# Attention with unscaled P and 1/sum broadcast through DRAM, in a one-core block of attention, RWKV-7 and a conv-FFN

## The chip, the cores and the metric

One core of a Trainium2 chip runs the whole kernel. The metric is the device time of one execution in microseconds; less is better. The engines are TensorE (PE, matmuls; PEld is its weight load), VectorE (DVE), ScalarE (ACT), GpSimd (POOL) and SyncE (SP, which here only issues DMAs). Each runs its own list of instructions in order, and waits at an instruction until what it needs is there.

## The reference

A block of a language model with 1024 tokens, width 1024, batch 1. What matters here is the mixer:

```
u = modulate(rms_norm(x), shift1, scale1)
proj = u @ w_in                                # fox: q, k, v, f | rwkv | 2 x 1024 gate columns
# 8 heads of 64
logits = q k^T * 64**-0.5 + cum[q] - cum[k]    # causal; cum = cumsum(log_sigmoid(f + b))
probs  = softmax(logits)
o_fox  = probs @ v
o_rwkv = rwkv7_time_mix(...)
merged = sigmoid(gate_fox) * (o_fox @ fox_w_out) + sigmoid(gate_rwkv) * (o_rwkv @ rwkv_w_out)
h = x + gate1 * (merged @ w_o)
u2 = modulate(rms_norm(h), shift2, scale2)
out = rms_norm(h + gate2 * conv_ffn(u2))
```

All in fp32.

## The kernel before

Products of fp32 matrices are made from a high and a low part of each operand (tiles `..hi`, `..lo`, type fp32r), in three matmuls: hi x hi, lo x hi, hi x lo. A weight comes by `load_w`: a DMA of 128x1024 into `raw`, a cast to `hi`, and a subtraction for `lo`. A gate (`w_in` 26 to 41, 16 of them) is computed in two halves of 512 tokens, 24 matmuls of 128x512 each, and its sigmoid is stored in DRAM (`d_gate`) until the branch products `br` want it.

The order on TensorE is written by a planner, `Weave`. Chains of work (Python generators) yield the time at which they wish to go on; a model of each engine's load (`weave.now`, `weave.use`) says when that is. Whenever no chain is due, the planner puts in a step of `weave.queue`: one matmul of a gate product. So the gates are the filler: 18 of their 32 halves stand ahead of the attention, 14 within it. `weave.late` is 0 before the attention, 1 within it, and 2 after. Inside the attention the order on DVE and ACT is that of the code as the planner walks it; SP and POOL are ordered by the scheduler.

In the attention, per head `h`, the queries are eight blocks `i` of 128 and are taken in pairs `I`:

- `load_head` brings three tiles by POOL's DMA queue: `stA` (parts of q and of k, 128 rows), `stB` (the other parts, 68 rows) and `vh` (v, high and low). There are two buffers of each; head 0 is loaded as the section begins, and each next one while its predecessor runs.
- `s_chain` makes the logits `lg` and spawns `softmax`: the negative maximum of a row on DVE (`nm`), Exp on ACT with the row's sum, then on DVE the reciprocal (128x1) and the scaling of P by it.
- `t_chain` transposes P on TensorE (`tp`), `halve` makes `th` (cast, ACT) and `tl` (subtraction, DVE), and `a_chain` multiplies with `vh` into one PSUM tile `ov`.
- `collect` adds the two halves of `ov` into `o` (a COPY on ACT, an addition on DVE). `o` holds two heads in its 128 rows, and 512 queries. When all is there, `fx` (its high and low parts, wanted by `br`) is written, by POOL for the heads 0 to 6, and by ACT and DVE for the last.
- `late_gate` and `gate_out` take one half of a gate at a time in the one PSUM tile `rk_ps`, and end in `gs` (two buffers, tag `sp0`, which the gates ahead of the section use too) and the store to `d_gate`. `weave.hold` keeps the filler away until `rk_ps` is read. The sigmoid is made of Abs, Relu, Exp, Ln, an addition on DVE and Exp, since Exp and Ln are in the table that ACT has loaded.

Later in the program `norm2` (lines L1358 and L1361, with Ln and Exp at L287 and L288) prepares the second norm in two halves; TensorE multiplies with its result `dg` at once (`tr`).

Of the kernel before, what the change touches and what calls it, by code (L numbers as in the profile page):

```python
# [16 lines left out]
S = 1024  # L17
# [114 lines left out]
def hybrid_block(ctx: ExitStack, tc: tile.TileContext, a, out):  # L132
# [41 lines left out]
    ident, ones = f32(eye_r), f32(C("ones"))  # L174
    epsr = cp.tile([128, 3], F32, name="epsr")
    nc.vector.memset(epsr[:, 2:3], 1e-37)
# [26 lines left out]
    d_st = dr.tile([8, 4, 128, S], F32R, name="d_st")  # L203
    d_v = dr.tile([8, 128, 8, 128], F32R, name="d_v")
    d_orw = dr.tile([4, 128, S], F32, name="d_orw")

# [38 lines left out]
    def load_w(src, name, pool=None, n=1024, scale=None, tags=("whi", "wlo"), bufs=2):  # L245

        pool = pool or wp
        raw = rp.tile([128, n], F32, tag="raw", name=f"raw_{name}")
        nc.sync.dma_start(raw, src)
        if scale is not None:  # L250
            nc.gpsimd.tensor_tensor(raw, raw, scale, op=ALU.mult)
        hi = pool.tile([128, n], F32R, tag=tags[0], name=f"hi_{name}", bufs=bufs)
        lo = pool.tile([128, n], F32R, tag=tags[1], name=f"lo_{name}", bufs=bufs)
        if weave.late == 1:
            i = nc.gpsimd.tensor_copy(hi, raw)
            if "head" in marks:
                tc.add_manual_dep(i.ins, marks["head"].ins.name, NOSYNC)
            for c in range(0, n, 256):
                nc.gpsimd.tensor_tensor(lo[:, c : c + 256], raw[:, c : c + 256], f32(hi[:, c : c + 256]), op=ALU.subtract)
        else:  # L260
            nc.scalar.copy(hi, raw)  # L261
            for c in range(0, n, NH):
                nc.vector.tensor_tensor(lo[:, c : c + NH], raw[:, c : c + NH], f32(hi[:, c : c + NH]), op=ALU.subtract)  # L263
        return hi, lo
# [752 lines left out]
    heads = {}  # L1017

    def load_head(h):
        A = at.tile([128, 2, S], F32R, tag="stA", name=f"stA{h}")  # L1020
        nc.gpsimd.dma_start(A, d_st[h, 0:2, :, :].rearrange("k r s -> r k s"))
        B = at.tile([128, 2, S], F32R, tag="stB", name=f"stB{h}")
        nc.gpsimd.dma_start(B[0:68, :, :], d_st[h, 2:4, 0:68, :].rearrange("k r s -> r k s"))
        vh = at.tile([128, 8, 128], F32R, tag="vh", name=f"vh{h}")
        i = nc.gpsimd.dma_start(vh, d_v[h])
        marks.setdefault("head", i)
        heads[h] = A, B, vh

    load_head(0)
    while len(weave.queue) > 12:  # L1030
# [5 lines left out]
    with tc.manual_schedule(engines={mybir.EngineType.DVE, mybir.EngineType.Activation}):  # L1036
        seq = [(h, I) for h in range(8) for I in ((0, 1, 3, 2) if h == 7 else (3, 0, 2, 1))]
        lg_free, tp_free, pl_free, ps_free, th_free, ov_free = (deque([0.0] * n) for n in (2, 2, 4, 2, 3, 1))
        probs, av_queue, halves = {}, deque(), {}
        ov_ps = pb.tile([128, NH], F32, tag="big", name="ov")[:, 0:256]  # L1040
# [7 lines left out]
        def s_chain():  # L1048

            yield 10500  # L1050
            for k, (h, I) in enumerate(seq):
                if k % 4 == 1 and h < 7:
                    load_head(h + 1)
                A, B, _ = heads[h]
                for i in (2 * I, 2 * I + 1):
# [8 lines left out]
                    for c0 in range(0, n, NH):  # L1064
                        c1 = min(n, c0 + NH)
                        mm(lg[:, c0:c1], A[:, 0, qs], A[:, 1, c0:c1], start=True, stop=False)
                        if c1 == n:
                            mm(lg[:, n - 128 : n], eye_r, tri_r, start=False, stop=False)
                        mm(lg[:, c0:c1], B[0:68, 0, qs], B[0:68, 1, c0:c1], start=False, stop=True)
                    weave.spawn(softmax(h, i, n, lg), 351)  # L1070
                    yield 0

        def softmax(h, i, n, lg):
            nm = at.tile([128, 3], F32, tag="nm", name=f"nm{h}_{i}", bufs=4)
            nc.vector.tensor_reduce(nm[:, 0:1], lg[:, 0:n], axis=AX.X, op=ALU.max, negate=True)  # L1075
# [3 lines left out]
            nc.scalar.activation(e[:, 0:n], lg[:, 0:n], AF.Exp, bias=nm[:, 0:1], accum_out=nm[:, 1:2])  # L1079
# [3 lines left out]
            yield t + 140 - weave.now  # L1083
            nc.vector.reciprocal(nm[:, 2:3], nm[:, 1:2])
            ts(e[:, 0:n], e[:, 0:n], nm[:, 2:3], None, op0=ALU.mult)
            t = weave.use("DVE", weave.now, 230 + 0.53 * n)
            probs[h, i] = t + 210, e

        def t_chain():
# [30 lines left out]
        def a_chain():  # L1120

            for _ in range(8 * 10):
# [4 lines left out]
                if jj == 0:  # L1127
                    yield from slot(ov_free)
                vh = heads[h][2]
                order = [(0, th), (1, th), (1, tl), (0, tl)] if jj == I else [(0, th), (0, tl), (1, th), (1, tl)]  # L1130
# [9 lines left out]
        def collect(h, I):  # L1140
# [11 lines left out]
            if len(got) == 4:  # L1152
                cs = slice(hf * NH, hf * NH + NH)
                if h < 7:
                    nc.gpsimd.tensor_copy(fx[0][p][:, cs], o)
                    nc.gpsimd.tensor_tensor(fx[1][p][:, cs], o, f32(fx[0][p][:, cs]), op=ALU.subtract)
                    return
# [8 lines left out]
        def late_gate(w, i):  # L1166
            for hf in range(2):
                cs = slice(hf * NH, hf * NH + NH)
                yield from gemm_steps(rk_ps, w, u, cs)
                weave.hold = weave.now + 1000  # L1170
                pending.append((i, hf))
# [3 lines left out]
        def gate_out(i, hf, cs):  # L1175

            g = gsp.tile([128, NH], F32, tag="sp0", name=f"gs{i}_{hf}")
            m = at.tile([128, NH], F32, tag="gm", name=f"gm{i}_{hf}", bufs=1)
            nc.scalar.activation(g, rk_ps, AF.Abs)
            nc.scalar.activation(m, rk_ps, AF.Relu, scale=-1.0)  # L1180
            weave.hold = weave.use("ACT", weave.now, 960) + 210
            nc.scalar.activation(g, g, AF.Exp, scale=-1.0)
            nc.scalar.activation(g, g, AF.Ln, bias=1.0)
            yield weave.use("ACT", weave.now, 960) + 140 - weave.now
            tt(g, g, m, op=ALU.add)
            yield weave.use("DVE", weave.now, 600) + 140 - weave.now
# [3 lines left out]
            pending.remove((i, hf))  # L1190

        def drain():
# [802 lines left out]
```

## Time and profile before

| what | us |
|---|---|
| median of three runs | 1701.07 (1699.76 to 1704.37) |
| the profiled execution | 1704.73 |
| its span, first to last instruction | 1703.0 |
| its mean granted TensorE clock | 0.983 |
| attention: first matmul into `rk_ps` to first `br` | 656.95 to 868.92 |

The profile is of one execution. Its page gives busy times by engine, the chain of work that ended last, groups of instructions (line, engine, operation, output<-input, shapes, count, then busy time, mean of one in ns, idle time ahead and what ended it) and DMA issues (count, size of one, median time from issue to landing). Other views: waits (engine, its work, what it waited for: total, times, longest), the instructions in order of time (start, length, engine, line, count; in brackets the idle time before it and what ended it) and stretches (for each engine busy time and, in brackets, instructions; then the granted clock of TensorE, the share of the DMA engines and GB/s). Neighbouring matmuls overlap in the listed lengths; their pitch is read from their starts.

### The profile page before, as it was taken

What the parts mean: (1) busy time and instruction counts of PE and PEld (TensorE: products, weight loads), DVE (VectorE), ACT (ScalarE), POOL (GpSimd) and SP (SyncE); (2) the same over time, 40 slices, a digit from 0 to 9 for tenths busy, and PEclk for the clock granted to TensorE, in tenths of its full rate; (3) what the DMA queues carried; (4) which work ended last, traced back from release to release, by engine and by line L of the source; (5) the groups of instructions that cost most, each with busy time, mean ns of one, the idle gap of its engine ahead of it and who ended that gap; (6) DMA issues with size and microseconds to landing.
All of it is one profiled execution on the core that took longest, in us unless ns stands there. A gap on an engine that the chain in (4) does not pass through costs nothing.

```text
span 1703.0 us, 26042 instructions
## 1 busy us (share of the span) xinstructions
PE 1638.0 (96%) x9772; PEld 1342.0 (79%) x9772; DVE 1220.8 (72%) x2390; ACT 808.6 (47%) x1482; POOL 143.4 (8%) x175
## 2 busy tenths in 40 slices
PE   5899999998999998999999999999999999999998
PEld 4767777786877776988878888888888888888886
DVE  5776787778676633888877634897777777787677
ACT  5453334333444554766642323654444444454455
POOL 0010101110111003123112000000000000000000
PEclk8899999999999999999999999999999999999999
DMA  8487743533342326433277611132333233484463
GB/s 328 139 314 205 192 125 97 136 106 106 91 115 75 91 81 151 141 110 107 76 265 268 246 62 63 50 105 94 123 107 103 93 117 101 163 284 153 125 215 112
DMA packets 120974, 239.85 MB, mean 141 GB/s; under 512 B 39888, under 2 KB 48336, under 8 KB 120848
## 3 DMA queue, kind: packets, MB, share of 16 engines
q1 hardware_dynamic: 112896, 220.94, 40.0%
q0 software_dynamic: 7952, 17.25, 3.8%
q8 instruction: 77, 1.26, 0.3%
q14 instruction: 49, 0.40, 0.1%
HBM read 172.59 MB, written 65.54 MB: 140 GB/s over the span
## 4 chain that ended last, share of the span: by engine, by line
PE 79%; DVE 9%; DMA 6%; ACT 2%; issue 2%; SPq 1%; DVEq 0%; ACTq 0%
PE X L140 13%; PE D L140 12%; PE Y L140 6%; PE wo L140 5%; PE br L140 5%; PE gt L140 5%; PE rk_ps L140 4%; PE qk L140 4%; PE ps_rkv L140 4%; PE W L140 3%; PE lg L140 2%; PE v L140 2%; PE ov L140 2%; PE sp L140 2%; PE tp L144 2%
## 5 line engine op out<-in xcount | busy, mean ns | idle before, releaser
L140 PE MATMUL D<-op,op 128*128 128x512 f32 x924 | 209.8, 390 | 0.0
L140 PEld LDWEIGHTS D<-op,op 128*128 128x128 f32 x924 | 173.5, 188 | 36.2 <-DVE op L1258 0.3
L140 PE MATMUL X<-T_m,S 128*128 128x512 f32 x440 | 107.3, 390 | 0.2
L140 PEld LDWEIGHTS X<-T_m,S 128*128 128x128 f32 x440 | 82.5, 188 | 18.2 <-ACT x L1534 0.6
L1257 ACT CAST op<-g 128x512 fp32r<-128x512 f32 x77 | 47.8, 621 | 74.1 <-PE D L140 48.0
L1258 DVE TENSOR_TENSOR op<-g,op 128x512 fp32r<-128x512 f32 x77 | 53.0, 689 | 41.7 <-ACT op L1257 41.7
L1494 DVE SCALAR_TENSOR_TENSOR c<-ab,vec,c 128x512 f32<-128x512 f32 x88 | 65.9, 750 | 19.5 <-ACT c L1497 17.9
L809 DVE TENSOR_TENSOR t<-E,M 128x60 f32<-128x60 f32 (+24 forms) x248 | 57.9, 233 | 30.2 <-DMA M<-sm 24.9
L1458 DVE TENSOR_TENSOR S<-ur,S 128x512 fp32r<-128x512 f32 x66 | 45.5, 691 | 35.6 <-ACT S L1454 35.5
L263 DVE TENSOR_TENSOR lo_in<-raw_in,hi_in 128x512 fp32r<-128x512 f32 x84 | 56.5, 707 | 16.1 <-PE gt L140 13.9
L1454 ACT CAST S<-ur 128x512 fp32r<-128x512 f32 x66 | 41.0, 622 | 55.6 <-DVE ur L1447 30.6
L1458 DVE TENSOR_TENSOR A<-ur,A 128x512 fp32r<-128x512 f32 x64 | 44.1, 688 | 30.9 <-ACT A L1454 30.7
L261 ACT CAST hi_in<-raw_in 128x1024 fp32r<-128x1024 f32 x42 | 44.0, 1049 | 44.3 <-PE ps_rkv L140 16.0
L140 PE MATMUL Y<-T_h,A 128*128 128x512 f32 x264 | 63.5, 390 | 0.0
L140 PE MATMUL Y<-T_h,S 128*128 128x512 f32 x264 | 63.3, 390 | 0.0
L140 PE MATMUL X<-B_b,A 128*128 128x512 f32 x252 | 60.8, 391 | 0.0
L140 PE MATMUL W<-B_f,A 128*128 128x512 f32 x252 | 60.6, 390 | 0.0
L1079 ACT ACTIVATE P<-lg,nm 128x896 f32<-128x896 f32 (+3 forms) x64 | 47.4, 743 | 22.8 <-DVE nm L1075 22.6
L811 DVE TENSOR_TENSOR E<-E,t 128x60 f32<-128x60 f32 (+24 forms) x248 | 53.8, 217 | 5.8
L140 PEld LDWEIGHTS Y<-T_h,A 128*128 128x128 f32 x264 | 49.6, 188 | 10.3
L140 PEld LDWEIGHTS Y<-T_h,S 128*128 128x128 f32 x264 | 49.6, 188 | 10.3
L1454 ACT CAST A<-ur 128x512 fp32r<-128x512 f32 x64 | 39.9, 623 | 34.2 <-PE X L140 31.5
(473 smaller groups left out, 4169.0 us busy)
## 6 DMA issues: line engine op xcount, KB each, us to landing
raw_in<-in_w_in SPq DMA_DIRECT2D x50, 512.0 KB, 3.7
wm<-in_w_mod SPq DMA_DIRECT2D x48, 512.0 KB, 7.0
ur<-in_w_up SPq DMA_DIRECT2D x44, 512.0 KB, 4.2
g<-d_g SPq DMA_DIRECT2D x35, 512.0 KB, 4.0
d_g<-gs SPq DMA_DIRECT2D x44, 256.0 KB, 2.0
d_g<-c SPq DMA_DIRECT2D x33, 256.0 KB, 4.4
d_st<-qh SPq DMA_DIRECT2D x64, 128.0 KB, 2.5
d_gate<-gs SPq DMA_DIRECT2D x32, 256.0 KB, 2.9
```

What stands on the lines that cost most here:

```text
L140: nc.tensor.matmul(o, lhsT, rhs, start=start, stop=stop, skip_group_check=more)
L144: nc.tensor.transpose(o, i, eye)
L261: nc.scalar.copy(hi, raw)
L263: nc.vector.tensor_tensor(lo[:, c : c + NH], raw[:, c : c + NH], f32(hi[:, c : c + NH]), op=ALU.subtract)
L809: tt(tv, E32[:, 0:J, s : s + 1].to_broadcast([128, J, W]), M32[:, s : s + 1, s + 1 : 32].to_broadcast([128, J, W]), op=ALU.mult)
L811: tt(E32[:, 0:J, s + 1 : 32], E32[:, 0:J, s + 1 : 32], tv, op=ALU.add)
L1079: nc.scalar.activation(e[:, 0:n], lg[:, 0:n], AF.Exp, bias=nm[:, 0:1], accum_out=nm[:, 1:2])
L1257: nc.scalar.copy(hi, src)
L1258: tt(lo, src, f32(hi), op=ALU.subtract)
L1454: nc.scalar.copy(hi, src)
L1458: tt(lo, src, f32(hi), op=ALU.subtract)
L1494: stt(c, ab[:, x + hf * NH : x + hf * NH + NH], V("conv_w", 22 * x + i), c, op0=ALU.mult, op1=ALU.add)
```

## The change

Seven edits:

1. `epsr` gets a fourth column that holds 0.5.
2. P stays unscaled. The four sums of a head's half (four blocks) go into one tile `sums`, with one reciprocal of 128x4; SP stores it in DRAM (`d_rs`) with the queries in a row, and loads it back as `R`, 512 queries broadcast to 64 rows. `collect` multiplies `o` by `R` on DVE, once for two heads and 512 queries.
3. A late gate is Tanh(x/2) and Identity(0.5 t + 0.5), both on ACT, and `hold` is 700 in place of 1000.
4. Weights loaded within the attention are split on ACT (cast) and DVE (two subtractions), not on POOL.
5. Head 0 is loaded by five DMAs into tiles of the pool `fxp`, and the two buffers of `stA`, `stB` and `vh` first hold heads 1 and 2; the first logits are due after 3500 ns by the planner's clock, not 10500.
6. POOL writes the low part of `fx` in two pieces of 256 columns.
7. The table of ACT is named ahead of the attention (`exp_and_others`) and after it (`use_ln_exp`).

```diff
@@ load_w
+        nc.scalar.copy(hi, raw)
         if weave.late == 1:
-            i = nc.gpsimd.tensor_copy(hi, raw)
...
-            for c in range(0, n, 256):
-                nc.gpsimd.tensor_tensor(lo[:, c : c + 256], ...)
-        else: ...
+            weave.use("ACT", weave.now, 900)
+            weave.use("DVE", weave.now, 1200)
+        for c in range(0, n, NH):
+            nc.vector.tensor_tensor(lo[:, c : c + NH], raw[:, c : c + NH], f32(hi[:, c : c + NH]), op=ALU.subtract)
@@ load of head 0
+    def load_first():
+        parts = [d_st[0, 0], d_st[0, 1], d_st[0, 2, 0:68, :], d_st[0, 3, 0:68, :], d_v[0].rearrange("p a x -> p (a x)")]
+        tiles = [fxp.tile([128, S], F32R, tag=f"h{t}", name=f"first{t}") for t in (3, 7, 2, 6, 5)]
+        for t, x in zip(tiles, parts):
+            marks["head"] = nc.gpsimd.dma_start(t[0 : x.shape[0], :], x)
+        heads[0] = *tiles[0:4], tiles[4].rearrange("p (a x) -> p a x", x=128)
...
-    load_head(0)
+    load_first()
@@ s_chain
-            yield 10500
+            yield 3500
@@ softmax
+            sm, done = sums[h, hf]
+            nc.scalar.activation(e[:, 0:n], lg[:, 0:n], AF.Exp, bias=nm, accum_out=sm[:, i % 4 : i % 4 + 1])
...
-            nc.vector.reciprocal(nm[:, 2:3], nm[:, 1:2])
-            ts(e[:, 0:n], e[:, 0:n], nm[:, 2:3], None, op0=ALU.mult)
+            if len(done) == 4:
+                nc.vector.reciprocal(sm[:, 4:8], sm[:, 0:4])
+                nc.sync.dma_start(d_rs[h, hf * NH : hf * NH + NH].rearrange("(i k) -> k i", k=128), sm[:, 4:8])
+                if h % 2 == 0:
+                    norms[p, hf] = at.tile([128, NH], F32, tag="R", name=f"R{p}{hf}", bufs=2)
+                nc.sync.dma_start(norms[p, hf][h % 2 * 64 : h % 2 * 64 + 64, :],
+                                  d_rs[h : h + 1, hf * NH : hf * NH + NH].to_broadcast([64, NH]))
@@ collect
             if len(got) == 4:
+                yield t - weave.now
+                tt(o, o, norms[p, hf], op=ALU.mult)
+                t = weave.use("DVE", weave.now, 600) + 140
@@ gate_out
-            nc.scalar.activation(g, rk_ps, AF.Abs)
-            nc.scalar.activation(m, rk_ps, AF.Relu, scale=-1.0)
-            nc.scalar.activation(g, g, AF.Exp, scale=-1.0)
-            nc.scalar.activation(g, g, AF.Ln, bias=1.0)
-            tt(g, g, m, op=ALU.add)
-            nc.scalar.activation(g, g, AF.Exp, scale=-1.0)
+            nc.scalar.activation(g, rk_ps, AF.Tanh, scale=0.5)
+            nc.scalar.activation(g, g, AF.Identity, scale=0.5, bias=epsr[:, 3:4])
@@ around the attention's run
+        nc.scalar.preload_act_table_set("exp_and_others")
         weave.run([a_chain(), t_chain(), s_chain()])
...
+    use_ln_exp()
```

Where the planner and the scheduler put it. First the start of the section on TensorE. A name's number tells buffers apart. Before, gate matmuls lead up to the first logits:

```order
L140 MATMUL rk_ps<-u_hi,hi_in_6764 128x512 x8
L140 MATMUL rk_ps<-u_lo,hi_in_6764 128x512 x8
L140 MATMUL rk_ps<-u_hi,lo_in_6765 128x512 x8
L140 MATMUL rk_ps<-u_hi,hi_in_6764 128x512 x8
L140 MATMUL rk_ps<-u_lo,hi_in_6764 128x512 x8
L140 MATMUL rk_ps<-u_hi,lo_in_6765 128x512 x3
L140 MATMUL lg_6_6952<-stA_6855 128x512
L140 MATMUL lg_6_6952<-stB_6857 128x512
```

Now, at the same place:

```order
L140 MATMUL rk_ps<-u_hi,hi_in_6766 128x512 x8
L140 MATMUL rk_ps<-u_lo,hi_in_6766 128x512 x8
L140 MATMUL rk_ps<-u_hi,lo_in_6767 128x512
L140 MATMUL lg_6_6922<-first_6858,first_6857 128x512
L140 MATMUL lg_6_6922<-first_6860,first_6859 128x512
L140 MATMUL lg_6_6922<-first_6858,first_6857 128x384
```

The logits of head 0 moved ahead by 26 gate matmuls. On ACT the place now reads (L328 is the last function of the last gate ahead of the section):

```order
L328 ACTIVATE gs_1_6886<-gs_1_6886 128x512
L1088 ACTIVATE P_6_6950,sums_1_6951<-lg_6_6922,nm_6_6934 128x896
L1198 ACT_TABLE_LOAD
L1198 ACTIVATE gs_0_6954<-rk_ps 128x512
L1200 ACTIVATE gs_0_6954<-gs_0_6954,epsr 128x512
L1088 ACTIVATE P_7_6958,sums_1_6951<-lg_7_6928,nm_7_6944 128x1024
```

The table comes in with the first Tanh, behind the first Exp of P; the two loads that the new calls name stand at the start of the whole program.

On DVE, the product with R for heads 0 and 1, second half of the queries, and what stands between it and the reciprocal of head 1 (rows left out in the middle are maxima, `tl` and `o` as these):

```order
L1163 TENSOR_TENSOR o_7119<-o_7119,ov 64x256
L1096 RECIPROCAL sums_1_7152<-sums_1_7152 128x4
L1130 TENSOR_TENSOR tl_30_7290<-tp_30_7261,th_30_7274 128x512
L1130 TENSOR_TENSOR tl_31_7294<-tp_31_7267,th_31_7279 128x512
L1130 TENSOR_TENSOR tl_32_7321<-tp_32_7302,th_32_7311 128x512
```

```order
L1130 TENSOR_TENSOR tl_10_7465<-tp_10_7437,th_10_7446 128x512
L1163 TENSOR_TENSOR o_7082<-o_7082,ov 64x256
L1080 TENSOR_REDUCE nm_0_7477<-lg_0_7461 128x1
L1130 TENSOR_TENSOR tl_11_7479<-tp_11_7452,th_11_7459 128x384
L1080 TENSOR_REDUCE nm_1_7481<-lg_0_7461 128x1
L1170 TENSOR_TENSOR o_7082<-o_7082,R_7055 128x512
L1080 TENSOR_REDUCE nm_4_7495<-lg_4_7471 128x1
```

The product is the 21st instruction behind its reciprocal. For the first half of the queries, with a reciprocal 12 rows later, the product stands 6 rows later than this one.

At the end, on TensorE, before:

```order
L140 MATMUL ov<-th_22_9211,vh_8625 128x256
L140 MATMUL ov<-th_22_9211,vh_8625 128x128
L140 MATMUL ov<-tl_22_9219,vh_8625 128x128
L140 MATMUL ov<-tl_22_9219,vh_8625 128x256
L140 MATMUL br_00_9297<-fx_6861,hi_br_9251 128x512
L140 MATMUL br_00_9297<-fx_6862,hi_br_9251 128x512
```

Now:

```order
L140 MATMUL ov<-th_22_9010,vh_8447 128x256
L140 MATMUL ov<-th_22_9010,vh_8447 128x128
L140 MATMUL ov<-tl_22_9015,vh_8447 128x128
L140 MATMUL ov<-tl_22_9015,vh_8447 128x256
L140 MATMUL rk_ps<-u_hi,hi_in_8612 128x512 x8
L140 MATMUL rk_ps<-u_lo,hi_in_8612 128x512 x8
```

Behind the last `ov` stand now three gate halves (one in `rk_ps`, two by the code of the gates ahead of the section), and then `br`.

More of the change, by code (lines that the diff above doesn't have):

```diff
@@ L174, in hybrid_block @@
     ident, ones = f32(eye_r), f32(C("ones"))
-    epsr = cp.tile([128, 3], F32, name="epsr")
+    epsr = cp.tile([128, 4], F32, name="epsr")
+    nc.vector.memset(epsr[:, 3:4], 0.5)
     nc.vector.memset(epsr[:, 2:3], 1e-37)
@@ L1169, in late_gate @@
                 yield from gemm_steps(rk_ps, w, u, cs)
-                weave.hold = weave.now + 1000
+                weave.hold = weave.now + 700
                 pending.append((i, hf))
@@ L1177, in gate_out @@
             g = gsp.tile([128, NH], F32, tag="sp0", name=f"gs{i}_{hf}")
[L1178 to L1186, printed above, removed]
-            nc.scalar.activation(g, g, AF.Exp, scale=-1.0)
+            nc.scalar.activation(g, rk_ps, AF.Tanh, scale=0.5)
+            weave.hold = weave.use("ACT", weave.now, 480) + 210
+            nc.scalar.activation(g, g, AF.Identity, scale=0.5, bias=epsr[:, 3:4])
             weave.use("ACT", weave.now, 480)
@@ L1190, in gate_out @@
             pending.remove((i, hf))
+            return
+            yield
         def drain():
```

40 lines of the change are left out of this document (19 added, 21 removed).

## The prediction

> **What bounds the kernel now.** I read the page first: the busy times and the chain that ended last.
>
> ```profile
> PE 1638.0 (96%) x9772; PEld 1342.0 (79%) x9772; DVE 1220.8 (72%) x2390; ACT 808.6 (47%) x1482; POOL 143.4 (8%) x175
> PE 79%; DVE 9%; DMA 6%; ACT 2%; issue 2%; SPq 1%; DVEq 0%; ACTq 0%
> ```
>
> TensorE is busy for 96% of the span. Only time in which it is idle or slow can be won, so relieving VectorE (DVE) or ScalarE (ACT) pays only where TensorE waits for them. Nearly all that the change touches lies in the attention section, from the first gate matmul into `rk_ps` (656.95 us) to the first branch matmul `br` (868.92 us). The view by stretches, whole section first, then the five places with losses:
>
> ```profile
> 657.00:869.00 212.00, 199.46 (x1202) 174.01 (x1200) 164.47 (x323) 140.44 (x318) 49.79 (x63) 0.97 0.41 114
> ...
> 660.00:670.00 10.00, 5.49 (x19) 4.14 (x18) 0.69 (x1) 3.32 (x6) 0.00 (x0) 0.82 1.15 249
> 670.00:680.00 10.00, 9.68 (x39) 7.55 (x39) 4.02 (x6) 3.32 (x7) 6.00 (x8) 0.84 0.39 88
> ...
> 730.00:750.00 20.00, 17.36 (x89) 14.33 (x88) 16.65 (x26) 10.40 (x23) 7.36 (x9) 0.83 0.48 136
> ...
> 830.00:850.00 20.00, 18.62 (x115) 16.15 (x114) 14.67 (x34) 12.95 (x33) 0.00 (x0) 1.00 0.04 14
> ...
> 860.00:870.00 10.00, 6.32 (x42) 5.11 (x42) 4.58 (x9) 6.90 (x14) 1.05 (x1) 1.00 0.52 168
> ```
>
> The columns are PE, PEld, DVE, ACT, POOL busy, then the granted clock. PE idles for 212.00 - 199.46 = 12.5 us, all of it in these five rows (4.5, 0.3, 2.6, 1.4, 3.7). The clock was granted at 0.82, 0.84 and 0.83 in three of them, which loses 1.8 + 1.6 + 3.4 = 6.8 us more. So 19.3 us of loss is visible: 8.2 at the start, 6.0 in 730 to 750, 1.4 in 830 to 850, 3.7 at the end. The waits of PE, and the rows at the start, in the middle and at the end:
>
> ```profile
> PE rk_ps L140 <- ACT gm L1180: 4.7, 2, 4.5
> PE ov L140 <- DVE o L1148: 3.2, 2, 2.2
> PE br L140 <- ACT hi_br L1231: 2.1, 1, 2.1
> ...
> 654.58 0.32 SPq L331 DMA_DIRECT2D d_gate<-gs  x1
> 656.95 1.98 PE L140 MATMUL rk_ps<-u_hi,hi_in 128*128 128x512 f32 x8
> 658.76 1.98 PE L140 MATMUL rk_ps<-u_lo,hi_in 128*128 128x512 f32 x8
> 665.92 0.60 ACT L1179 ACTIVATE gs<-rk_ps 128x512 f32<-128x512 f32 x1 [5.46 <-DMA d_gate<-gs]
> 667.06 2.50 PE L140 MATMUL rk_ps<-u_hi,hi_in 128*128 128x512 f32 x5 [4.51 <-ACT gm L1180]
> ...
> 736.54 0.89 PEld L144 LDWEIGHTS tp<-cst,P 128*128 128x128 f32 x8
> ...
> 737.10 1.29 POOL L1156 TENSOR_TENSOR fx<-o,fx 128x512 fp32r<-128x512 f32 x1
> 737.69 3.66 DVE L1085 TENSOR_SCALAR P<-P,nm 128x384 f32<-128x384 f32 x1
> 738.34 2.79 POOL L259 TENSOR_TENSOR lo_in<-raw_in,hi_in 128x256 fp32r<-128x256 f32 x4
> 741.86 0.69 PE L140 MATMUL ov<-th,vh 128*128 128x256 f32 x2 [2.22 <-DVE o L1148]
> ...
> 866.88 0.37 ACT L1146 COPY o<-ov 64x256 f32<-64x256 f32 x1 [1.52 <-PE ov L140]
> 868.92 2.11 PE L140 MATMUL br<-fx,hi_br 128*128 128x512 f32 x8 [2.08 <-ACT hi_br L1231]
> ```
>
> At the start the gate's output tile waits for its slot: the `d_gate` write of 654.58 lands only at 665.9, while the loads of two heads fill the DMA engines (1.15 busy, 249 GB/s). In the middle one P scale, at 3.66 us, runs exactly as long as GpSimd (POOL) subtracts beside it, and PE waits for the `o` behind it. At the end there is no TensorE work left between the last `ov` and `br`.
>
> The section has a third loss, too short for a wait. Eight matmuls of 512 columns start 658.76 - 656.95 = 1.81 us apart, 0.226 each or 0.443 ns a column. Without any gap the section would be 336 gate matmuls, 76.1 us, and per head 19,456 columns of logits and P-times-V (8.6 us) and 36 transposes at 0.89 / 8 = 0.11 (4.0 us), for eight heads 101 us: 177 in all, 35 below 212. About 7 of this is structural, an estimate: matmuls of 128 columns (0.057 us by the pitch, but a weight load each of about 0.11). So some 28 us could be won: 19 visible and about 9 in short gaps all over the section.
>
> **The change, part by part.** The costs on DVE and ACT, by groups within the section (the first row is all scales of P, busy time and count):
>
> ```profile
> 657.00:869.00 212.00, 40.18 (x64) 0.97 0.41 114
> ...
> L1185 DVE TENSOR_TENSOR gs<-gs,gm 128x512 f32<-128x512 f32 x14 | 10.7, 767 | 14.0 <-ACT gs L1183 13.8
> L1084 DVE RECIPROCAL nm<-nm 128x1 f32<-128x1 f32 x64 | 10.0, 156 | 2.9 <-ACT P L1079 2.7
> ...
> L1182 ACT ACTIVATE gs<-gs 128x512 f32<-128x512 f32 x14 | 9.0, 640 | 0.0
> ...
> L261 ACT CAST hi_in<-raw_in 128x1024 fp32r<-128x1024 f32 x42 | 44.0, 1049 | 44.3 <-PE ps_rkv L140 16.0
> L263 DVE TENSOR_TENSOR lo_in<-raw_in,hi_in 128x512 fp32r<-128x512 f32 x84 | 56.5, 707 | 16.1 <-PE gt L140 13.9
> ```
>
> DVE loses 40.2 (P scales), 10.7 (gate sums) and 48 of 64 reciprocals (7.5); it gains 12 weight halves at 0.71 (8.5) and eight products with R at about 0.7 (5.6). Net -44 us: 164 falls to 120. ACT runs two functions of about 0.63 for a gate half in place of five, and 12 halves in place of 14: 43.5 falls to 15; six casts at 1.05 add 6.3. Net -22: 140 falls to 118. POOL loses the weights' casts and subtractions. The work of TensorE is the same, but two whole gates and two halves change place: 72 of the 336 gate matmuls now stand behind the last `ov` (24 in `rk_ps`, 48 in the next section), so 264 fill the attention and 72 x 0.226 = 16.3 us cover the last output's way into `fx`. With 190 us of TensorE time, DVE and ACT stand at about 62% each, where DVE was at 78%.
>
> What I expect to be left of the 28 us:
> - Start: 8.2 falls to 3. The first logits stand behind 17 gate matmuls, not 43, but the gate's first Tanh still needs the slot that `d_gate` frees, and now three heads load at once. ACT has one Exp ahead of it.
> - 730 to 750: 6.0 falls to 0. No scale of P and no weight subtraction on POOL is left to meet.
> - 830 to 850: 1.4 falls to 0.5, as the load of DVE.
> - End: 3.7 falls to 0.7. The output chain is covered by the 72 matmuls; what stays is a `hi_br` cast that stands on ACT behind the gates' last functions (one function of 0.63).
> - Short gaps: 9 falls to 4.5, taking half for DVE's fall by a quarter and a chain two operations shorter for each block.
>
> Left 8.7, won 19.5. The gates' `hold` and the half-width `fx` writes on POOL I cost at nothing: both lie under the gate matmuls.
>
> The new wait is R. Each reciprocal tile goes out as 2 KB in pieces of 4 bytes and comes back to 64 rows. The nearest round trips:
>
> ```profile
> sm<-E SPq DMA_DIRECT2D x32, 32.0 KB, 1.7
> ...
> M<-sm SPq DMA_DIRECT2D x32, 128.0 KB, 3.5
> ...
> d_gate<-gs SPq DMA_DIRECT2D x32, 256.0 KB, 2.9
> ...
> stB<-d_st POOLq DMA_DIRECT2D x8, 544.0 KB, 12.8
> ```
>
> A quiet one is two issues of 0.32 and landings of 1.7 and 3.5: 5.8 us. From above, two like `stB`, 25.6 us. I take 6 to 7, since the `sm` rows are the same kind of small store and reload on the same queue. On DVE the product with R stands 20 and 14 instructions behind its reciprocal, at 0.4 to 0.7 us each 9 to 13 us: covered, so 0 in the sum. The 32 new issues on SP (0.32 each, 10 us in 190) also hold the raw weight loads and gate stores behind them while SP waits for a reciprocal; a gate's weights are wanted only every 48 matmuls (10.8 us). If the cover is gone, DVE stands at the product, and the maxima and the `tl` behind it, for which ACT and then PE wait.
>
> Tables of ACT. `exp_and_others` is now active from the first Tanh on, and what follows needs Ln. One gate is left for the old chain (two halves, four loads) and each of the two blocks of norm2 gets two. The rows:
>
> ```profile
> 1492.33 1.28 ACT L197 ACT_TABLE_LOAD   x1
> 1493.62 0.62 ACT L1257 CAST op<-g 128x512 fp32r<-128x512 f32 x1
> ...
> 1009.25 0.20 ACT L288 ACTIVATE ssq<-ssq 128x4 f32<-128x4 f32 x1
> 1016.66 1.61 PE L140 MATMUL tr<-dg,h_sb 128*128 128x128 f32 x13
> ...
> 1060.77 0.30 ACT L287 ACTIVATE ssq<-ssq,epsr 128x4 f32<-128x4 f32 x1 [0.23 <-DVE ssq L1358]
> 1061.34 0.88 DVE L1361 TENSOR_SCALAR dg<-cst,ssq 128x128 f32<-128x128 f32 x4 [0.60 <-ACT ssq L288]
> 1061.98 2.28 PE L140 MATMUL tr<-dg,h_sb 128*128 128x128 f32 x19
> ```
>
> A load takes 1.28 us and the next instruction starts 0.01 later. The first norm2 has 7 us between its Exp and the `tr` that needs it, which hides two loads. In the second one `tr` follows directly: 2 x 1.29 = +2.6 us. The gate's four loads stand under matmuls with four PSUM banks: 0. The Trainium skill, page "ScalarE: Activation LUTs", section "What ACT_TABLE_LOAD costs", adds a drain of about 1.38 us to each load, 2.66 us a switch; the rows above show no such gap, and by the page's figure the second norm2 would cost 5.3 us, the time 2.7 more.
>
> Two more loads at the very start push the first Squares, whose last one waits for data anyway: 0.1.
>
> Sum: -19.5 + 2.6 + 0.1 = -16.8 us. The profiled execution took 1704.73 us (span 1703.0), so 1687.9; it is 3.7 above the median of the three runs, 1701.07, and against that the time is **1684.3 us**.
>
> **The rivals.**
> 1. *The start stays as it was.* For it: three heads' loads stand in the queue where two jammed it, and a `d_gate` write took 11.3 us. Against: the logits need only four of the five first tiles, in order. Price: the start keeps 8.2 and 2 on top, 7 more than taken: 1691.
> 2. *The filler was what hid the gaps.* With 264 gate matmuls in place of 336 (16 us fewer) the short chains lg, max, Exp, tp, th, tl, ov show as PE waits. For it: the rows of `ov` waiting for `o` and `th`. Against: DVE and ACT at 62%. The short gaps stay at 9 and another 4 us appear: 1684 + 8.5 = 1693.
> 3. *R comes late; slower than before.* Place: the eight products on DVE. Price: with a round trip of 14 us, the even halves stand 4 to 5 us and the odd ones 1 to 2, four times each, 24 us, and each stand over 2 us of PE brings a stretch at half clock as after 741.86 (3.4 us lost), four of them 13.6. It loses the gain and ends at 1684 + 37 = 1721. It decides from a round trip of about 12 us; below 9 it costs nothing. For it: raw weights and gate stores share SP's queue; a `stB` takes 12.8. Against: `sm` and `M` rows.
> 4. *Table loads cost more than their length.* The second norm2 lets PE stand for 2.6 us; a wait of 2.2 in 741.86 was followed by half clock, one of 2.08 ahead of `br` was not. With the half clock 3.4 more, 1688.
> 5. *All short gaps go*, since nothing but DVE made them: 4.5 and 2 of the start more, 1678.
>
> The lock between DVE and POOL could come back with the products: the Trainium skill, page "SBUF — State Buffer", section "Who interferes with whom", says that a DVE operation with two inputs in SBUF and a GpSimd one block each other as whole instructions. The P scale of 3.66 us fits that it blocks; with `fx` written in pieces of 256 columns (2.79 / 4 = 0.7 us) a product would stand for one of them at most, on an engine with slack.
>
> **How the numbers follow.** Forecast (1679 to 1690, the error of the start, the gaps and the table loads) 0.50; rival 1 0.14; rival 2 0.12; rival 3 0.07; rival 4 0.09; rival 5 0.08. 0.3% is 5 us, about what a measurement of this kernel can tell from no change. Rival 3 gives slower 0.07; halves of rival 2 and a late R of 10 to 12 us give the same, 0.08; the rest is faster, 0.85. Range: from rival 5 with its own error, 1674, to rival 2's upper side, 1696.
>
> **What would show it.** Right: `ov` no longer waits for `o` at the place of POOL's subtractions; a clock of 1.00 in the middle of the section; no PE idle ahead of `br`; DVE about 120 us and ACT 118 in it; no idle of DVE ahead of the products with R on DMA; two loads ahead of the second norm2's Ln and Exp and a PE wait of 2 to 3 us at `tr`. Wrong: DVE rows "<-DMA R"; PE rows waiting for `th` or P; an idle PE of over 4 us at the start. The forecast fails first if the round trip of R exceeds 9 us or if the gate slot comes later than now.

## The result

The changed kernel takes 1760.62 us (median of 4 runs, 1758.07 to 1765.64) against 1700.41 before: a ratio of 1.0358, 95% interval [1.0324, 1.0392]. It is 60 us slower, where 16.8 us faster had been forecast. It is the third rival, R late through DRAM, and dearer than that rival's 1721.

The profile after, in the parts that answer to those shown of before. First the page's busy times and chain that ended last, then the section from the first `rk_ps` to the first `br` (PE, PEld, DVE, ACT, POOL busy, clock, DMA share, GB/s):

```profile
PE 1655.1 (94%) x9772; PEld 1356.0 (77%) x9772; DVE 1182.8 (67%) x2287; ACT 812.1 (46%) x1461; POOL 122.5 (7%) x153
PE 69%; DMA 12%; DVE 10%; issue 3%; ACT 3%; SPq 2%; DVEq 0%; ACTq 0%; POOL 0%; POOLq 0%
...
654.70:926.10 271.40, 213.91 (x1202) 187.01 (x1201) 128.53 (x221) 131.03 (x284) 31.60 (x41) 0.87 0.53 107
```

The section grew from 212.0 to 271.4 us. DVE is busy for 128.5 us (164.5 before, forecast 120) and ACT for 131.0 (140.4 before, forecast 118), but PE idles 57 us, and its mean granted clock is 0.87 where it was 0.97. DMA, with 6% of the chain before, has 12%, half of it one small store, `d_rs<-sums`. The waits within the section, of PE, DVE, SP and ACT:

```profile
PE ov L140 <- DVE tl L1130: 25.5, 4, 8.0
PE lg L140 <- ACT P L1088: 12.6, 4, 9.2
PE tp L144 <- DVE tl L1130: 11.4, 3, 4.7
PE lg L140 <- DMA stB<-d_st: 6.1, 1, 6.1
...
DVE o L1170 <- issue: 48.9, 6, 16.1
DVE o L1170 <- DMA R<-d_rs: 7.8, 2, 7.5
...
SPq L1101 <- DMA d_rs<-sums: 193.0, 16, 24.0
...
ACT P L1088 <- DMA d_rs<-sums: 15.8, 2, 11.6
```

Read from below: SP, which issues the loads of R (L1101), spends 193 us of the section waiting for the 16 stores of 2 KB, 12 us each. DVE, in order, stands 56.7 us ahead of the eight products (L1170); for 48.9 of them the profile names no releaser (`issue`), and it is the experiments that tie them to R. Behind it stand the `tl`, for which PE's `ov` and `tp` wait 37 us. ACT waits too: the Exp writes its sums into one of three `sums` tiles, and a tile is free only when its store has landed. One such store, out for 24.8 us (SP's issues in the order of time), and then one such stand of DVE, at another place:

```profile
742.65 0.73 SPq L1098 DMA_DIRECT2D d_rs<-sums  x1
767.46 0.45 SPq L1101 DMA_DIRECT2D R<-d_rs  x1
...
718.39 0.95 DVE L1080 TENSOR_REDUCE nm<-lg 128x1 f32<-128x768 f32 x1
729.80 0.69 DVE L1170 TENSOR_TENSOR o<-o,R 128x512 f32<-128x512 f32 x1 [10.46 <-issue]
```

And the transfers of the section with their median time to landing:

```profile
stA<-d_st POOLq DMA_DIRECT2D x7, 1024.0 KB, 12.9
d_gate<-gs SPq DMA_DIRECT2D x15, 256.0 KB, 10.2
stB<-d_st POOLq DMA_DIRECT2D x7, 544.0 KB, 23.2
...
R<-d_rs SPq DMA_DIRECT2D x16, 128.0 KB, 6.9
...
d_rs<-sums SPq DMA_DIRECT2D x16, 2.0 KB, 10.8
```

The smallest transfer is among the slowest. A round trip is 10.8 + 0.45 + 6.9 = 18 us, not 6 to 7, and the others are slower too: `stA` took 6.0 us before, `d_gate` 2.9.

### The profile page after: what moved, and what is told of

Read it like the earlier page. It is cut to its first block, busy times and chain, and to the rows that moved or that the text cites. A ratio compares the mean times of both kernels' runs of the same rounds, so it can differ in the third digit from the quotient of the medians.

```text
span 1763.9 us, 25999 instructions
## 1 busy us (share of the span) xinstructions
PE 1655.1 (94%) x9772; PEld 1356.0 (77%) x9772; DVE 1182.8 (67%) x2287; ACT 812.1 (46%) x1461; POOL 122.5 (7%) x153
## 4 chain that ended last, share of the span: by engine, by line
PE 69%; DMA 12%; DVE 10%; issue 3%; ACT 3%; SPq 2%; DVEq 0%; ACTq 0%; POOL 0%; POOLq 0%
PE X L140 12%; PE D L140 12%; DMA d_rs<-sums 6%; PE Y L140 6%; PE gt L140 6%; PE br L140 5%; PE wo L140 5%; PE ps_rkv L140 4%; PE W L140 3%; PE qk L140 3%; PE rk_ps L140 2%; PE sp L140 2%; PE v L140 1%; DMA wm<-in_w_mod 1%; PE low L140 1%
## 5 line engine op out<-in xcount | busy, mean ns | idle before, releaser
L261 DVE TENSOR_TENSOR lo_in<-raw_in,hi_in 128x512 fp32r<-128x512 f32 x96 | 65.3, 714 | 21.9 <-PE gt L140 14.0
L256 ACT CAST hi_in<-raw_in 128x1024 fp32r<-128x1024 f32 x48 | 50.2, 1048 | 44.4 <-PE ps_rkv L140 16.2
L1475 DVE TENSOR_TENSOR S<-ur,S 128x512 fp32r<-128x512 f32 x66 | 45.5, 691 | 35.7 <-ACT S L1471 35.5
L1080 DVE TENSOR_REDUCE nm<-lg 128x1 f32<-128x896 f32 (+3 forms) x64 | 47.4, 752 | 28.5 <-PE lg L140 25.5
L1130 DVE TENSOR_TENSOR tl<-tp,th 128x512 fp32r<-128x512 f32 (+1 forms) x80 | 50.2, 633 | 23.6 <-ACT th L1127 17.8
L140 PE MATMUL ov<-tl,vh 128*128 128x256 f32 (+1 forms) x140 | 38.8, 322 | 25.5 <-DVE tl L1130 25.5
L144 PE MATMUL tp<-cst,P 128*128 128x128 f32 x288 | 48.3, 297 | 11.4 <-DVE tl L1130 11.4
```

Of the source, the lines that this page charges most:

```text
L140: nc.tensor.matmul(o, lhsT, rhs, start=start, stop=stop, skip_group_check=more)
L144: nc.tensor.transpose(o, i, eye)
L1080: nc.vector.tensor_reduce(nm, lg[:, 0:n], axis=AX.X, op=ALU.max, negate=True)
L1130: tt(tl[:, 0:w], tp[:, 0:w], f32(th[:, 0:w]), op=ALU.subtract)
L1475: tt(lo, src, f32(hi), op=ALU.subtract)
```

## The experiments

The before runs beside them had medians of 1699.8 to 1700.6. Times of one version differ from its median by up to 7 us, part of it ahead of the section, which starts between 651 and 660 us; so each run is also read by the length of its section, first `rk_ps` to first `br`, which held all 336 gate matmuls in each profile.

| run | what it is | time, us | ratio to before, 95% | section, us |
|---|---|---|---|---|
| before | | 1700.4 | | 212.0 |
| e11_before_again | before, unchanged | 1697.3 (one run) | | 209.6 |
| after | the whole change | 1760.6 | 1.0324 to 1.0392 | 271.4 |
| e1_no_product | after, no product with R | 1739.4 | 1.0191 to 1.0259 | 235.9 |
| e2_p_scaled | after, P scaled, no R | 1698.4 | 0.9973 to 0.9993 | 205.1 |
| e3_store16 | after, 128 pieces of 16 bytes | 1697.7 | 0.9962 to 0.9990 | 205.6 |
| e4_rows_by_pe | after, 4 pieces of 512 bytes | 1699.9 | 0.9983 to 1.0011 | 204.9 |
| e5_own_lines | after, 512 pieces, 8 bytes apart | 1720.1 (one run) | | 222.2 |
| e6_8byte | after, 256 pieces of 8 bytes | 1698.7 (one run) | | 208.0 |
| e7_tables_tied | e4, tables in place | 1699.5 | 0.9982 to 1.0008 | 205.7 |
| e8_old_start | e4, old start | 1704.1 | 1.0017 to 1.0038 | 209.0 |
| e9_weights_only | before, weights on ACT and DVE | 1718.9 | 1.0091 to 1.0117 | 228.8 |
| e10_p_scaled_tied | e2, tables in place | 1697.9 | 0.9967 to 0.9993 | 206.8 |
| e13_store16_tied | e3 with queries right, tables in place | 1695.9 | 0.9963 to 0.9991 | 204.8 |
| f3_tanh_only | before, Tanh gates, tables in place | 1693.2 | 0.9945 to 0.9974 | 204.3 |
| f2_tanh_r16 | f3 and R with 16-byte stores | 1698.3 | 0.9974 to 0.9999 | 207.1 |
| f1_weights_on_pool | e13, weights on POOL again | **1690.5** | 0.9925 to 0.9958 | 199.9 |
| f4_p_scaled_pool | f1, P scaled, no R | 1694.3 | 0.9945 to 0.9976 | 202.5 |

### Where the 60 us are

First, the product taken out, with the transfers left in:

```diff
-                tt(o, o, norms[p, hf], op=ALU.mult)
-                t = weave.use("DVE", weave.now, 600) + 140
+                t = weave.now
```

> The changed kernel without the multiplication of o by R on DVE (outputs stay unscaled); the stores of the reciprocals and the loads of R stay as they are. Theory A (the store of 4-byte pieces lands after 9 to 25 us, and DVE, in order, stands at the eight products until R is there): the 57 us of DVE's wait ahead of the products are gone, the time falls to 1685 to 1700. Theory B (the 32 transfers themselves do the harm: they hold SP's queue and slow the loads of heads, gate stores and weights behind them, stA 12.9 us in place of 6.0): the time stays above 1740. Theory C (neither; the rest of the change, with fewer gate matmuls in the section, lost the time): no change, 1760.

Neither theory alone: 1739.4, right between. Without the product the time falls by 21 us of the 60, and 39 stay with no reader of R at all. The section by itself falls by 35.5 of 59.4 us, but some of that is lost again behind it, where `br` waits 9.2 us for a part of its weight (the third row, behind the first `br`). This run's waits of PE and of ACT say where the rest goes:

```profile
PE lg L140 <- ACT P L1088: 18.0, 5, 7.7
PE lg L140 <- DMA stB<-d_st: 11.6, 2, 11.1
PE br L140 <- ACT hi_br L1247: 9.2, 1, 9.2
...
ACT P L1088 <- DMA d_rs<-sums: 22.0, 3, 10.4
ACT hi_br L1247 <- DMA raw_br<-in_w_br: 6.0, 1, 6.0
```

The store holds the `sums` tiles, so ACT's Exp and then the logits; and it holds SP, and slows the loads of the next heads and weights. Next, scales of P back on DVE, no R:

```diff
+            nc.vector.reciprocal(sm[:, 4 + i % 4 : 5 + i % 4], sm[:, i % 4 : i % 4 + 1])
+            ts(e[:, 0:n], e[:, 0:n], sm[:, 4 + i % 4 : 5 + i % 4], None, op0=ALU.mult)
...
-                tt(o, o, norms[p, hf], op=ALU.mult)
...
```

> The changed kernel with P scaled on DVE block by block as before, and no store of reciprocals, no R, no product; all other parts of the change stay (Tanh gates, weights split on ACT and DVE, head 0 by five loads, earlier logits). Theories A and B: 1685 to 1695, since the start, the lock with POOL and the end are mended without R; head loads back at about 6 us. Theory C: still above 1720.

1698.4, and `stA` back at 5.5 us: R is all of the loss. The rest of the change, without the unscaled P, brings 2 us; the whole had been forecast to bring 17. Then the same R with another store:

```diff
-                nc.sync.dma_start(d_rs[h, hf * NH : hf * NH + NH].rearrange("(i k) -> k i", k=128), sm[:, 4:8])
+                nc.sync.dma_start(d_rs[h, hf * NH : hf * NH + NH].rearrange("(k i) -> k i", i=4), sm[:, 4:8])
```

> The changed kernel with the reciprocals stored as 128 pieces of 16 bytes, one for a partition, in place of 512 pieces of 4 bytes; the same 2 KB at the same place, the queries of a half then stand in another order, so the outputs are wrong. If the landing goes by the number of pieces (theory A1), it falls from 10.8 to about 3 us and the time to 1690 to 1705. If it is a fixed price of a small store to DRAM or of its place in the queue (theory A2), the landing stays at 9 to 11 us and the time near 1755.

1697.7: the whole loss is gone, with the same 32 transfers, the same bytes, the same products. So it is the pieces, not the number of transfers (theory B as stated falls). With rows turned on TensorE:

```diff
+                tp = pt.tile([128, NH], F32, tag="tp", name=f"rt{h}_{hf}")
+                transpose(tp[0:4, 0:128], sm[:, 4:8], ident)
...
+                row = at.tile([4, 128], F32, tag="row", name=f"row{h}_{hf}", bufs=1)
+                nc.scalar.copy(row, tp[0:4, 0:128])
...
+                nc.sync.dma_start(d_rs[h, hf * NH : hf * NH + NH].rearrange("(i k) -> i k", k=128), row)
```

> The changed kernel with the four reciprocals of a block turned to four rows of 128 queries by one small transpose on TensorE (128x4 to 4x128, through a tp buffer), copied by ACT and stored as 4 pieces of 512 bytes; R and the products stay. Theory A1: the store lands in about 2 us as the 32 KB sm stores did, R follows in 3.5, the products find R there, and the time is 1685 to 1695, close to the run without the product. Theory A2: the store still takes 9 us or more and the time stays above 1740. Theory B: above 1730, since the transfers are as many.

1699.9, 5 us above what was expected of it, though no product waits for R. Two experiments on the place and the size of the pieces:

```diff
+                nc.sync.dma_start(d_rs[h, hf * S : hf * S + S].rearrange("(k i x) -> k i x", i=4, x=2)[:, :, 0], sm[:, 4:8])
...
```

> The changed kernel with its 512 pieces of 4 bytes stored 8 bytes apart, the four of one partition side by side in DRAM, in place of 4 bytes apart with the 128 partitions side by side; R then loads other values (outputs wrong). If the landing goes by the number of 4-byte pieces (theory A1), it stays at 9 us and more and the time near 1760. If it is the place in DRAM (neighbouring partitions, carried by different DMA engines, write into the same few bytes and wait for each other: theory A3), it falls to 2 to 4 us and the time to about 1700.

```diff
+                nc.sync.dma_start(d_rs[h, hf * NH : hf * NH + NH].rearrange("(j k i) -> k j i", k=128, i=2), sm[:, 4:8].rearrange("k (j i) -> k j i", i=2))
```

> The changed kernel with 256 pieces of 8 bytes in place of 512 of 4 (outputs wrong, queries out of order). In quiet moments the store took 9.0 us at 512 pieces and 1.4 at 128. By number alone (theory A1, a fixed 1.2 and some 15 ns a piece) it takes 4 to 5 us at least, and the time lies at 1705 to 1725. By the place of neighbours (theory A3), it depends on how many partitions share a place: half as many, 4 to 5 us too. If only 4-byte pieces are slow (theory A4), about 1.5 us and 1698.

The landings of the store as each profile gives them (lowest, median, highest), with 512 pieces of 4 bytes, 512 pieces 8 bytes apart, 256 of 8 bytes and 128 of 16 bytes, in this order:

```profile
DMA to landing us min/median/max: 9.0/10.8/24.8
...
DMA to landing us min/median/max: 3.8/6.5/13.5
...
DMA to landing us min/median/max: 2.8/10.0/12.6
...
DMA to landing us min/median/max: 1.4/7.3/12.2
```

And SP's waits for those stores in each section (total, times, longest), in the same order and with the four rows of 512 bytes last:

```profile
SPq L1101 <- DMA d_rs<-sums: 193.0, 16, 24.0
...
SPq L1102 <- DMA d_rs<-sums: 107.5, 16, 13.1
...
SPq L1101 <- DMA d_rs<-sums: 92.3, 16, 12.2
...
SPq L1101 <- DMA d_rs<-sums: 65.9, 16, 11.7
...
SPq L1108 <- DMA d_rs<-row: 25.5, 15, 7.1
```

12.1, 6.7, 5.8, 4.1 and 1.7 us a store. The medians among the landings are less use: SP issues R straight behind the store that it waits for, and by its rows the medians from the one issue to the other are 10.9, 6.1, 4.6 and 2.3 us, and 1.2 for the four rows.

Both the place and the size of the pieces count. At the same number and size, another place takes the store from 9.0 to 3.8 us in the quietest case, so theory A1 alone falls; the time, 1720.1, stays 20 us above what theory A3 had. The place changed in two ways, in the distance of the pieces and in whose piece lies beside whose, and these were not taken apart. With half and a quarter of the pieces it falls on to 2.8 and 1.4. For the 8-byte store none of the three theories is right: the 2.8 lies between their 1.5 and 4, while the time, 1698.7, is that of theory A4. Why neighbours at 4 bytes are so slow stays open; the order of the pieces in time was not tried apart from their place. At 16 bytes ten of the 16 stores took under 4 us and the other six 7 to 12; of these, five went out 3 to 5 us behind the loads of a head, and the first 15 us behind those of two heads. The products waited 4.7 us in all.

### Where the 17 us went

The start, undone on e4:

```diff
-    load_first()
+    load_head(0)
...
-            yield 3500
+            yield 10500
```

> The kernel with rows by TensorE, with the old start: head 0 by load_head and the first logits due after 10500. If the start's stall is what the new loads mended (5.2 us by the prediction), the time rises from 1699.9 to about 1705, with an idle TensorE of 4 us and half clock near 665 us. If the stall came with the gate's slot and not with the loads, it is the same, 1699 to 1701.

1704.1: the start is worth 4.2 us, and the section differs by as much. The wait came back where it had been, now ahead of a table load and a Tanh (PE, in the waits of this run):

```profile
PE rk_ps L140 <- ACT gs L1205: 7.3, 5, 4.5
```

The tables, each load tied to the ACT instruction ahead of its place, on e4, and then on e2:

```diff
+        tc.add_manual_dep(i.ins, marks["act"].ins.name, NOSYNC)
...
+    use_ln_exp(marks["act"])
```

> The kernel with rows by TensorE, with the two table loads tied to the last ACT instruction of the gates ahead of them, so that one stands ahead of the attention and one behind its last gate, and the last gate's two halves by Tanh as well. Eight loads fewer. If the two loads in the second norm2 are the 2.4 us by which everything behind the first br took longer (836.4 in place of 834.1 us), the stretch from br to the end returns to about 834 and the time falls from 1699.9 to 1697.5. If the loads are hidden there and the 2.3 us are of another cause, no change, 1699.9.

> The kernel with P scaled on DVE (no R; 1698.4), with the table loads tied to their place and the last gate by Tanh, as in the run with tied tables. If the two loads ahead of the second norm2 are a price that every execution pays, 1696; if not, 1698.4.

Inconclusive in time: 1699.5 and 1697.9, each within noise of its partner. The wait ahead of the second norm2 (1.9 us, shown below) is gone in the profile of e7. From the first `br` to the end the profiled executions take 834.1 us before, 836.2 to 836.8 in the six versions with untied loads and no wait at `br` (e2 to e6, e8), and 832.3 to 835.9 in the seven with tied ones. In the two highest of these (e7 and f1) a stretch at a granted clock of 0.50 near 960 us lasts longer and costs 1.7 us more than in the others that were read there (e4, e13). So a price of about 2 us is there, but a median does not show it.

Before again, since the lock might have been the luck of one execution:

> The kernel before, unchanged, profiled a second time. Theory L: the 6.0 us lost in 730 to 750 (a scale of P of 3.66 us beside POOL) are not there again, the start's 8 us are. Against it: both losses stand at the same places.

It is not. The second profile has the same scale of P, and the same wait behind it, while the start's wait is 3.5, not 4.5:

```profile
L1085 DVE TENSOR_SCALAR P<-P,nm x64: 285/554/3659, 670.6 to 850.1; 128x896 f32<-128x896 f32 x8, 128x1024 f32<-128x1024 f32 x8, 128x128 f32<-128x128 f32 x8, 128x256 f32<-128x256 f32 x8
...
PE rk_ps L140 <- ACT gm L1180: 3.8, 2, 3.5
PE ov L140 <- DVE o L1148: 3.2, 2, 2.2
```

Its cure, alone on the kernel before:

```diff
+        nc.scalar.copy(hi, raw)
         if weave.late == 1:
-            i = nc.gpsimd.tensor_copy(hi, raw)
...
+            weave.use("ACT", weave.now, 900)
+            weave.use("DVE", weave.now, 1200)
+        for c in range(0, n, NH):
+            nc.vector.tensor_tensor(lo[:, c : c + NH], raw[:, c : c + NH], f32(hi[:, c : c + NH]), op=ALU.subtract)
```

> The kernel before with one part of the change: weights loaded within the attention are split on ACT and DVE, not on POOL. If the lock of POOL and DVE in 730 to 750 is a loss that every execution has (6.0 us in the prediction's sum), the time falls from 1700 to 1694 to 1696. If it was the luck of the one profiled execution (theory L), or if DVE at 78% has no room for 8 us more, the time stays at 1699 to 1702.

1718.9, slower by 18 us. The long scale is gone (the longest 1.86 us), and PE waits more (section, and its waits):

```profile
654.30:883.10 228.80, 206.37 (x1202) 177.69 (x1200) 168.15 (x336) 145.87 (x323) 25.27 (x31) 0.96 0.37 105
...
PE ov L140 <- DVE tl L1111: 6.4, 7, 1.8
PE rk_ps L140 <- ACT gm L1176: 6.0, 4, 3.8
PE lg L140 <- ACT P L1075: 2.9, 5, 1.1
PE tp L144 <- DVE P L1081: 2.4, 1, 2.4
```

DVE and ACT are busy only 4 and 5 us more, but the new work stands in their order between the `tl`, the maxima and the Exp that PE needs. The edit also enters that work in the planner's model (`weave.use`), so the order of everything else moves with it; how the 18 us divide between the two was not tried. Then the 16-byte stores with the queries put right and the tables tied, and on top of that the weights taken back to POOL:

```diff
+                ov = o.rearrange("p (i k) -> p i k", k=128)
+                tt(ov, ov, norms[p, hf].rearrange("p (k i) -> p i k", i=4), op=ALU.mult)
```

> The changed kernel with the reciprocals stored as 128 pieces of 16 bytes, R loaded in that order, and the product on DVE reading R with a stride that puts the queries right; tables tied and the last gate by Tanh. As the run with 16-byte pieces (1697.7) less 2.4 for the tables: 1695, if DVE reads R at a stride of 16 bytes as fast as in a row (0.69 us). If the stride doubles the product, the time is the same, since DVE has room.

> The last version (16-byte stores, R read with a stride, tables tied; 1695.9 us) with the weights of the attention split on POOL as before. Theory W (the split on ACT and DVE costs more in their queues than the lock it ends; alone it cost 18 us): faster, 1688 to 1692, with no operation of DVE beyond 1.5 us, since no scale of P is left to be locked out. Theory L2 (the lock comes back with the products and the tl): a DVE operation of 3 us or more again and 1698 to 1702.

e13 has 1695.9, as expected, though the strided product took 1.09 us, not 0.69. f1, with POOL's split back, has 1690.5: the fastest version, 0.9941 of before [0.9925, 0.9958]. The lock did not come back: no `tl`, product or maximum takes over 1.3 us. The section of f1 and its waits of PE:

```profile
654.00:853.90 199.90, 192.87 (x1202) 169.93 (x1200) 122.82 (x208) 122.55 (x275) 53.20 (x71) 1.00 0.54 148
...
PE ov L140 <- DVE o L1172: 2.5, 2, 2.2
PE ov L140 <- DVE tl L1139: 1.7, 1, 1.7
PE rk_ps L140 <- ACT gs L1208: 1.6, 3, 0.7
```

Last, the gates alone, R on top of them, and P scaled in f1:

> The kernel before with the Tanh gates alone (hold 700, tables tied, last gate by Tanh). ACT has 28 us and DVE 11 us less. If the waits of PE for ACT and DVE go down with their load, 1694 to 1697; the wait at the first gate stays, since it ends with the slot's store. If not, 1699 to 1701.

> The kernel before with the Tanh gates (tables tied) and the unscaled P with 16-byte stores and R; start and weights as before. DVE is relieved of 45 us and has no scale of P that POOL could lock out. If relief of DVE and the lock's end are worth what the prediction had (6.0 and part of 4.5 and 3.0), 1689 to 1693. If what the relief frees is only slack, 1698 to 1701.

> The version with weights on POOL (1690.5) with P scaled on DVE block by block as before, and no R. Start, Tanh gates and tied tables stay. If unscaled P brings what DVE is relieved of (37 us), this is slower: 1694 to 1698, with the lock back at a scale of P. If DVE has room for the scales and R only adds transfers and a wait, as the runs with Tanh gates alone and with R added to them say (1693.2 and 1698.3), 1687 to 1691.

The Tanh gates alone bring 6.6 us (1693.2), where 3 to 6 were forecast by load. They also end the lock, although P is still scaled on DVE and the weights are still split on POOL. Here is the row of the scales in f3, and the middle of its section:

```profile
L1091 DVE TENSOR_SCALAR P<-P,nm x64: 285/588/1503, 678.2 to 843.1; 128x896 f32<-128x896 f32 x8, 128x1024 f32<-128x1024 f32 x8, 128x128 f32<-128x128 f32 x8, 128x256 f32<-128x256 f32 x8
...
720.00:740.00 20.00, 19.08 (x119) 16.53 (x118) 18.22 (x36) 12.34 (x29) 7.18 (x8) 1.00 0.40 119
740.00:760.00 20.00, 19.87 (x133) 17.78 (x132) 15.44 (x33) 13.05 (x32) 5.08 (x7) 1.00 0.46 135
```

These 40 us lose 1.0 us; in the second profile of before they lost 6.0 (2.6 idle, 3.4 by a clock of 0.85 and 0.98). So most of the gain of the Tanh gates may be the lock's, which ended because the order shifted; one profile of each cannot say more. In f4 the longest scale takes 1.34 us, so the lock that was expected there did not come back either.

R on top of the Tanh gates costs 5 us (1698.3), and yet R in f1 gains 4 over scales of P (1694.3); the 4 are the less certain, as the intervals of f1 and f4 overlap. So the parts do not add: what unscaled P is worth turns with the order around it. Each of these edits also changes what the planner does, and why the worth turns was not settled.

## Why the prediction was wrong, point by point

- *R.* The step that failed is "I take 6 to 7, since the `sm` rows are the same kind of small store". They were not: what counted was the pieces, 4 bytes side by side, and the text had named them and still priced them by a store of 32 KB that landed in 1.7. The store measured 10.8 (9.0 to 24.8) and R 6.9. With that, "covered, so 0 in the sum" fell too, by about 60 us. For longer pieces the price would have held: with 16 bytes (e3) the pair takes 2.3 + 0.45 + 3.1 = 5.9 us. The bound from above, 25.6 for the pair, held the 18 measured. The rival's turning point of 12 us is not borne out: e5, with 6.1 + 0.5 + 3.7 = 10.3 in the median, already takes 22 us more than e3.
- *Rival 3's price.* It counted only DVE's standing and half clock (37 us). Taking the product out wins 21 us (e1). The other 39 also come with the store, since they go when it is stored in longer pieces (e3); the waits point to the `sums` tiles, SP's queue and slowed loads, which the price had left out, and do not divide the 39 among them. Nor does every stand of PE over 2 us bring half clock: f1 has one of 2.2 us and a mean granted clock of 1.00 in its section.
- *Start.* Forecast 5.2, measured 4.2 (e8 against e4). Right.
- *End.* Right: the first `br` starts straight behind the last gate matmul.

```profile
924.24 1.98 PE L140 MATMUL gt<-u_hi,lo_in 128*128 128x512 f32 x8
926.05 1.98 PE L140 MATMUL br<-fx,hi_br 128*128 128x512 f32 x8
```

- *Tables.* Right in place and about in size: +2.6 forecast; behind the first `br` 2.1 to 2.7 us more with untied loads than before (3.8 in the changed kernel itself), and this wait in the profile after, with the first of the two loads ahead of it.

```profile
1119.17 1.28 ACT L285 ACT_TABLE_LOAD   x1
1122.66 2.61 PE L140 MATMUL tr<-dg,h_sb 128*128 128x128 f32 x21 [1.90 <-DVE dg L1378]
```

  A load here takes 1.28 us, and the two delay `tr` by 1.9, less than their length. By the 2.66 us a switch of the Trainium skill's page "ScalarE: Activation LUTs", section "What ACT_TABLE_LOAD costs", an estimate for the two is 5.3, and that does not appear.
- *Lock, 6.0 to 0.* The long scale and its loss are real and recur in the unchanged kernel (e11). But they come from an encounter in the order and not from scaling P beside POOL as such: f3 and f4 do both and have no scale over 1.50 us. That it is a lock is inferred from the times, which fit only roughly: the scale ran from 737.69 to 741.35, POOL's two operations beside it from 737.10 to 741.13. And the cure was counted as free. The split of weights on ACT and DVE, with the order that comes with it, costs 5.4 us in the best version (e13 against f1) and 18 alone. The forecast put their 8.5 and 6.3 us into the engines' sums and never asked who stands behind them.
- *Short gaps, 9 to 4.5.* Not won at all. Before, PE was busy 199.5 us with 6.8 of it lost to half clock: 192.7 at full clock. f1 has 192.87 at clock 1.00, e4 197.15 with its 16 transposes, f4 193.9. DVE's load fell from 164 to 123 us between before and f1 and won none of the 9, so "some 28 us could be won" was too much by about as many; whether another order could win them is not shown.
- *PE's idle.* Left in e4: 204.90 - 197.15 = 7.8 us, where the four visible places had 4.2 left. The waits move to `tl` and `o` at other places.
- *DVE and ACT.* DVE came near its forecast (128.5 us busy, 120 forecast). ACT did not (131.0, 118 forecast): the two halves by the old code of the gates, with two more table loads, stand inside the section and take 5.1 + 2.6 us of it, where before had 2.4 us of such work. And a lower load did not by itself shorten the waits: in f2 DVE is busy for 35 us less than in f3 (121.8 and 156.4), and PE idles 11.2 us in its section against 9.2.

## What to carry to other kernels

Price a small transfer by its pieces: a transposing store of 512 words of 4 bytes cost 9 to 25 us, the same 2 KB in runs of 16 bytes 1.4 to 12, mostly under 4, and the reader can take the permuted order with a stride. A wait that is hidden by its reader's distance still holds its buffer and its queue: ask who writes that buffer next and what is issued behind it. Work put on an engine that has idle time can cost what stands behind it in that engine's order, so try each part alone: here one part gained 6.6 us, one cost 18, and the best version, 0.9941 of before, keeps the change but for its store, its weights and its untied tables. A long operation that recurs at the same place may still be an encounter of two engines that any shift of the order ends; before pricing its cure, see whether it needs one.

## What the runs showed of the hardware

- A store of 2 KB in 512 neighbouring pieces of 4 bytes landed after 9.0 us at the least, 8 bytes apart after 3.8, as 256 pieces of 8 after 2.8, as 128 of 16 after 1.4. By SP's issues the medians of the 16 stores are 10.9, 6.1, 4.6 and 2.3.
- While such stores were out, others landed late: `d_gate` in 10.2 us, with 2.2 in e3, and `stA` in 12.9, with 7.9 in e3.
- A DVE product of 128x512 in fp32 that reads one of its two operands at a stride of 16 bytes takes 1.09 us (e13, f1), with both in a row 0.69.
- A table load that is not tied to an instruction can end at the program's start, where the next load undoes it: the changed kernel has three loads in a row there.
